# Three one-row reads between the loads and the stores of a rotary-embedding kernel

## The chip, the cores and the metric

One core of a Trainium2 chip runs the kernel. The metric is the device time of the program in microseconds; each kernel was run several times, always beside the kernel before on the same chip. All runs told of here are of the fast state. A ratio is the mean time of one kernel's fast runs over that of the other kernel's fast runs of the same rounds, so it is not quite the ratio of the medians that I quote. The profile of a kernel shows one of its executions; its span (83.6 us before) is shorter than the device time (85.28 us); it is counted from the program's first instruction to its last.

## The reference

```python
# x: [8, 8, 1024, 64] float32; cos_cached, sin_cached: [1024, 32] float32
half = x.shape[-1] // 2
x_first, x_second = x[..., :half], x[..., half:]
out_first  = x_first * cos_cached - x_second * sin_cached
out_second = x_first * sin_cached + x_second * cos_cached
return concatenate([out_first, out_second], axis=-1)
```

16.8 MB go in and 16.8 MB come out; the tables are 128 KB each.

## The kernel before

x is cut into 8 units of 128 partitions x 4096 floats (2 MB). All units have their own place in SBUF, so every load can be issued at once, and every store goes out from the place where its unit was loaded and computed. VectorE (DVE in the profiles) makes most of the products, GpSimd (POOL) and TensorE (PE) make most of the sums, ScalarE (ACT) copies into and out of PSUM. What the change touches is the list of SP, the engine that issues nearly all transfers. What SP has issued and the 16 DMA engines have yet to move is called its ring (q1 in the profiles):

```python
nc.sync.dma_start(out=rs, in_=sin_cached...)       # SP
nc.scalar.dma_start(out=rc, in_=cos_cached...)     # ACT, its own ring
for m0, m1 in ((0, F // 2), (F // 2, F)):          # unit 0 in two halves
    nc.sync.dma_start(out=xt[0][:, m0:m1], in_=xf[0][:, m0:m1])
for u in range(1, n_u):
    nc.sync.dma_start(out=xt[u], in_=xf[u])
# ... compute; as units are ready, in this order:
# store(0), store(1), ... store(6), then unit 7 in three parts
def store(u, n0=0, n1=R):
    nc.sync.dma_start(out=of[u][:, n0*hd:n1*hd], in_=xt[u][:, n0*hd:n1*hd])
```

The framework gives each of these transfers one of eight completion semaphores in turn. Before it reuses one it makes the issuing engine wait until the transfer eight places earlier has landed. The instruction lists of the traces show this wait at the issues; the source does not.

## Time and profile before

| | before |
|---|---|
| device time, median of the first 3 runs | 85.28 us (85.21 to 85.71) |
| span of the profile | 83.6 us |
| last load of x landed | 43.37 us |
| last compute instruction ended (POOL) | 75.5 us |
| last store landed | 82.62 us |
| share of 16 DMA engines' time used by SP's ring | 95.5% |

Read it from the bottom row up: the ring is what is full, and it still runs 7 us after the last engine has finished. The prediction below shows the lines. To them I add SP's own waits (columns: who waited, for whom, us in total, times, longest), of the kernel before (three dots: lines left out):

```profile
SPq L142 <- POOL w L110: 39.3, 8, 12.1
SPq L142 <- DVE w L106: 13.3, 3, 9.7
SPq L142 <- ACT w L190: 12.3, 2, 7.2
...
SPq L83 <- DMA w<-in_x_dram: 1.5, 1, 1.5
```

SP waits for most of the span, nearly always for compute (L142 is the store).

### The profile page before, as it was taken

Reading aid. Unit: us, or ns where it says so; the run is one execution under the profiler, and the core shown is the slowest. Engines: PE = TensorE matmul, PEld = TensorE weight load, DVE = VectorE, ACT = ScalarE, POOL = GpSimd, SP = SyncE. Lnnn points to the kernel's source line nnn. Section 1 sums busy time; section 2 is a strip of 40 time slices with the busy share of each in tenths; the row PEclk is TensorE's granted clock in tenths of the full one; section 3 lists DMA queues with packets and bytes.
Section 4 is the critical chain, followed back from the end, with each engine's and each line's share of the span. In section 5 each row is a group of like instructions: output and inputs, shape, how many; then the busy total and the mean of one; then the engine's idle time right before and its main releaser. Section 6 shows DMA issues by size and latency. Waiting matters only on the chain.

```text
span 83.6 us, 386 instructions
## 1 busy us (share of the span) xinstructions
PE 44.1 (53%) x80; PEld 16.9 (20%) x80; DVE 68.5 (82%) x30; ACT 40.7 (49%) x36; POOL 67.2 (80%) x36
## 2 busy tenths in 40 slices
PE   0199930004993694949769494961994970000000
PEld 0143300002430332405133240411340410000000
DVE  0193999999999999999999999999999998940000
ACT  4409694464068548196176856675266526000000
POOL 3009909999999999999999999999999999991000
PEclk9999999999999999999999999999579999655555
DMA  1999999999999999999999898999999999999990
GB/s 18 308 415 447 435 431 447 392 470 407 423 447 407 454 400 439 439 415 447 384 423 454 384 486 384 478 400 454 423 400 470 392 478 392 470 400 394 423 425 20
DMA packets 2833, 33.82 MB, mean 404 GB/s; under 512 B 337, under 2 KB 337, under 8 KB 785
## 3 DMA queue, kind: packets, MB, share of 16 engines
q1 hardware_dynamic: 2784, 33.69, 95.5%
q10 hardware_dynamic: 48, 0.13, 0.4%
q14 instruction: 1, 0.00, 0.0%
HBM read 17.04 MB, written 16.78 MB: 404 GB/s over the span
## 4 chain that ended last, share of the span: by engine, by line
POOL 63%; issue 13%; PE 4%; DMA 4%; DVE 3%; POOLq 2%
POOL w L109 26%; POOL w L110 24%; POOL w L106 14%; PE en L156 4%; DMA w<-in_sin_cached_dram 4%; DVE w L106 3%; POOLq L258 2%; POOLq L109 0%; POOLq L106 0%
## 5 line engine op out<-in xcount | busy, mean ns | idle before, releaser
L106 DVE TENSOR_TENSOR w<-st,tb 128x3072 f32<-128x3072 f32 (+2 forms) x19 | 54.7, 2956 | 0.3 <-ACT st L113 0.3
L113 ACT COPY st<-w 128x1536 f32<-128x1536 f32 (+1 forms) x19 | 24.9, 1310 | 15.7 <-DVE w L106 14.6
L184 PE MATMUL acc<-w,plus 128*128 128x512 f32 x36 | 21.4, 679 | 20.4 <-ACT w L190 11.4
L109 POOL TENSOR_TENSOR w<-w 128x1024 f32<-128x1024 f32 (+3 forms) x11 | 23.9, 2169 | 0.2
L110 POOL TENSOR_TENSOR w<-w 128x1024 f32<-128x1024 f32 (+3 forms) x11 | 23.8, 2166 | 0.0
L184 PEld LDWEIGHTS acc<-w,plus 128*128 128x128 f32 x36 | 6.9, 215 | 33.9 <-ACT w L190 18.0
L190 ACT COPY w<-acc 128x1024 f32<-128x1024 f32 x9 | 9.1, 1010 | 8.5 <-PE acc L185 8.5
L106 POOL TENSOR_TENSOR w<-w,tb 128x1280 f32<-128x1280 f32 x4 | 11.7, 2921 | 0.2
L185 PE MATMUL acc<-w,minus 128*128 128x512 f32 x18 | 10.9, 690 | 0.0
L185 PE MATMUL acc<-w,plus 128*128 128x512 f32 x18 | 9.2, 592 | 0.0
L162 POOL COPY tb<-tb 32x2048 f32<-32x2048 f32 x2 | 3.8, 1888 | 5.2 <-DVE tb L159 5.2
L156 PE MATMUL en<-w,sel 32*128 32x512 f32 x4 | 3.7, 1089 | 3.9 <-DMA w<-in_sin_cached_dram 3.9
L185 PEld LDWEIGHTS acc<-w,minus 128*128 128x128 f32 x18 | 4.0, 223 | 5.4 <-issue 5.4
L106 DVE TENSOR_TENSOR w<-pre,tb 128x4096 f32<-128x4096 f32 x1 | 4.4, 4418 | 0.0
L185 PEld LDWEIGHTS acc<-w,plus 128*128 128x128 f32 x18 | 3.4, 190 | 4.4 <-issue 4.4
L109 POOL TENSOR_TENSOR w<-w,w 128x1024 f32<-128x1024 f32 x1 | 2.4, 2361 | 2.2 <-issue 2.2
L156 PE MATMUL ec<-w,sel 32*128 32x512 f32 x4 | 3.6, 1056 | 0.0
L160 ACT COPY tb<-tb 32x2048 f32<-32x2048 f32 x1 | 1.9, 1897 | 3.4 <-DVE tb L159 3.4
L106 DVE TENSOR_TENSOR w<-w,en 128x2048 f32<-128x2048 f32 x1 | 2.3, 2289 | 1.4 <-PE en L156 1.4
L159 DVE LOAD_MASK_SELECT tb<-w x2 | 0.0, 8 | 3.8 <-DMA w<-in_sin_cached_dram 3.8
L159 DVE STREAM_SHUFFLE tb<-w 32x1024 f32<-32x1024 f32 x2 | 2.5, 1282 | 0.0
L106 DVE TENSOR_TENSOR w<-w,ec 128x1024 f32<-128x1024 f32 x2 | 2.4, 1218 | 0.0
(18 smaller groups left out, 14.2 us busy)
## 6 DMA issues: line engine op xcount, KB each, us to landing
w<-in_x_dram SPq DMA_DIRECT2D x7, 2048.0 KB, 24.9
out_dram<-w SPq DMA_DIRECT2D x7, 2048.0 KB, 10.5
w<-in_x_dram SPq DMA_DIRECT2D x2, 1024.0 KB, 6.4
out_dram<-w SPq DMA_DIRECT2D x2, 768.0 KB, 6.7
out_dram<-w SPq DMA_DIRECT2D x1, 512.0 KB, 6.7
w<-in_cos_cached_dram ACTq DMA_DIRECT2D x1, 128.0 KB, 3.3
w<-in_sin_cached_dram SPq DMA_DIRECT2D x1, 128.0 KB, 3.1
```

Source lines behind the costliest of these rows:

```text
L106: eng.tensor_tensor(out=o, in0=a, in1=t, op=TT.mult)
L109: eng.tensor_tensor(out=o[:, :, 0], in0=c[:, :, 0], in1=s[:, :, 1], op=TT.subtract)
L110: eng.tensor_tensor(out=o[:, :, 1], in0=c[:, :, 1], in1=s[:, :, 0], op=TT.add)
L113: nc.scalar.copy(out=pt[:, :(n1 - n0) * hd], in_=xt[u][:, n0 * hd:n1 * hd])
L156: nc.tensor.matmul(part, sel, r, start=True, stop=True)
L159: nc.vector.stream_shuffle(t[0:Q, H:], flat(r), odd)
L160: nc.scalar.copy(out=tb4[Q:2 * Q, H:], in_=tb4[0:Q, H:])
L162: nc.gpsimd.tensor_copy(out=tb4[k * Q:(k + 1) * Q, H:], in_=tb4[0:Q, H:])
L184: nc.tensor.matmul(a[:, k], plus, xr[:, :, k], start=True, stop=False)
L185: nc.tensor.matmul(a[:, k], plus if k else minus, sr[:, :, 1 - k], start=False, stop=True)
L190: nc.scalar.copy(out=rows(xt[u], n0, n0 + G), in_=a)
L258: with _tile.TileContext(nc) as tc:
```

## The change

The three reads bring a row of 64 floats each into a small buffer that nobody uses. They do no work for the result. They cost three small transfers and shift the semaphores of all stores by three places.

```diff
     for u in range(1, n_u):
         nc.sync.dma_start(out=xt[u], in_=xf[u])
+
+    row = const.tile([1, 3 * hd], fp32, name="row")
+    for i in range(3):
+        nc.sync.dma_start(out=row[:, i * hd:(i + 1) * hd], in_=xf[i][0:1, 0:hd])
```

## The prediction

> **What bounds the kernel now.** I read the page first, from its DMA lines. They say that the queues are never empty.
>
> ```profile
> DMA  1999999999999999999999898999999999999990
> GB/s 18 308 415 447 435 431 447 392 470 407 423 447 407 454 400 439 439 415 447 384 423 454 384 486 384 478 400 454 423 400 470 392 478 392 470 400 394 423 425 20
> ...
> q1 hardware_dynamic: 2784, 33.69, 95.5%
> ...
> HBM read 17.04 MB, written 16.78 MB: 404 GB/s over the span
> ```
>
> Each digit is one fortieth of the span, 2.09 us. Apart from the first and the last slice the 16 DMA engines are busy in tenths 8 or 9 all the way, and SP's ring (q1) alone fills 95.5% of 16 engines' time. The chain of waits names another engine:
>
> ```profile
> POOL 63%; issue 13%; PE 4%; DMA 4%; DVE 3%; POOLq 2%
> ```
>
> That chain starts from the last instruction of a compute engine, and POOL's last work ends at 75.5 us of a span of 83.6 us. The stretch view shows what is left after that (columns: stretch, length, busy us of PE, PEld, DVE, ACT and POOL, granted clock, DMA share, GB/s):
>
> ```profile
> 43.00:48.00 5.00, 3.90 (x10) 1.62 (x9) 5.00 (x3) 3.57 (x4) 5.00 (x4) 1.00 0.98 419
> 53.00:58.00 5.00, 2.79 (x7) 0.95 (x5) 5.00 (x2) 3.52 (x3) 5.00 (x3) 1.00 1.05 449
> 63.00:68.00 5.00, 3.90 (x10) 1.44 (x8) 5.00 (x3) 2.36 (x2) 5.00 (x3) 1.00 0.98 419
> 73.00:78.00 5.00, 0.00 (x0) 0.00 (x0) 1.15 (x2) 0.00 (x0) 2.51 (x2) 0.50 0.99 423
> 78.00:82.60 4.60, 0.00 (x0) 0.00 (x0) 0.00 (x0) 0.00 (x0) 0.00 (x0) 0.50 0.81 334
> ```
>
> From 78 us on no compute engine works, and the DMA engines still run until 82.6 us. The bound is therefore the transfer stream: 9 loads of x, then 10 stores, on one ring. The compute engines matter only if they hand a store over so late that the ring runs dry. The issues of the stores and their times to landing say whether they do:
>
> ```profile
> 21.76 0.35 SPq L142 DMA_DIRECT2D out_dram<-w  x1
> 35.39 0.34 SPq L142 DMA_DIRECT2D out_dram<-w  x1
> 47.90 0.33 SPq L142 DMA_DIRECT2D out_dram<-w  x1
> 63.90 0.33 SPq L142 DMA_DIRECT2D out_dram<-w  x1
> 69.51 0.33 SPq L142 DMA_DIRECT2D out_dram<-w  x1
> 75.53 1.35 SPq L142 DMA_DIRECT2D out_dram<-w  x2
> ```
> ```profile
> DMA to landing us min/median/max: 5.8/9.5/26.4
> ```
>
> The store issued at 21.76 us takes 26.4 us to land although 2 MB need only about 4.9 us: it stands behind the loads. From the trace's records of the completion semaphores I take each landing. Loads of unit 0 (two halves) 6.62 and 9.10, units 1 to 7 at 13.99, 18.88, 23.78, 28.67, 33.57, 38.46, 43.37 us; stores of units 0 to 6 at 48.20, 53.12, 58.04, 62.96, 67.89, 72.80, 77.70 us; the three parts of unit 7 at 79.54, 81.38, 82.62 us. That is one full transfer each 4.89 us (loads) or 4.92 us (stores), without a hole. A store is issued before the one ahead of it has landed by: 43.37 - 21.76 = 21.6, 48.20 - 35.39 = 12.8, 53.12 - 47.90 = 5.2, 5.5 (issue 52.51), 5.8 (57.12), 4.0 (63.90), 3.3 (69.51), 5.7 (72.03), 4.0 (75.53), 5.4 us (75.96). The smallest slack is 3.3 us, at unit 6. A new transfer needs about 1.1 us from issue to its first packet (the sine table: issue 0.74, first packet 1.79), so some 2.2 us of it are real.
>
> **What the Trainium skill says.** "DMA: Bandwidth & Descriptors", section "Anatomy of one DMA": the DMA engines do not wait on semaphores; a wait is held by the issuing sequencer before dispatch. The trace agrees: SP's waits stand ahead of its issues, and loads that were issued by 6.96 us move until 43.37 us. Same page, "Queues, rings and completion order": on each DMA engine descriptors are consumed in ring order. The 26.4 us of the first store agree. Same page, "Specifications": a fabric ceiling of 435 GB/s for 16 engines. Here 2.097 MB in 4.89 us is 429 GB/s, so there is nothing to gain from more in flight. Same page, "Why a DMA increments its semaphore by 16 and not by 1": a transfer runs on k engines, k at most 16 and set by the slowest dimension that is not 1. A row of 64 elements may then go as one 256 B packet on one engine or as 16 pieces of 16 B; no record of the kernel before shows which.
>
> **The change part by part.** Nothing is removed. The compute engines have the same instructions in the same order, with the same waits. SP's list gains three issues after the ninth load, and the completion semaphores are shifted by that: there are eight, handed out in the order of issue (the cosine table on ACT's queue included), and each issue first waits for the transfer eight places earlier. 21 transfers become 24.
>
> (a) Waits before the reads. They wait for the second half of unit 0 (9.10 us), unit 1 (13.99) and unit 2 (18.88), so SP issues them then. SP has nothing else to do: its first store is ready at 21.76 us. Cost 0.
>
> (b) Waits before the stores. Before, the stores of units 0 to 4 waited for the loads of the second half of 0, then 1 to 4. Now they wait for the loads of units 3, 4, 5, 6 and 7, landing at 23.78, 28.67, 33.57, 38.46 and about 43.4 us. Against the issue times 21.76, 35.39, 47.90, 52.51 and 57.12 us only the first is held up, by 23.78 - 21.76 = 2.0 us, and that store has 21.6 us of slack. The stores of units 5 and 6 and the first part of 7 wait for the three reads (landed by about 44 us; issues at 63.90, 69.51, 72.03). The last two parts wait for the stores of units 0 and 1, as before (landed 48.2 and 53.1; issues 75.5 and 76.0). Cost 0.
>
> (c) Bytes in the ring. The reads are issued after the last load (6.63 us) and so lie between it and the first store, at about 43 us, in the stream that sets the end. The trace's packets give the size: 4096 B take 159 ns, 16384 B 611 ns (medians), so 452 ns for 12288 B, or 0.0368 ns a byte, and 159 - 151 = 8 ns fixed. A 256 B packet is then an estimated 8 + 9.4 = 17 ns, its semaphore packet 9 ns (mean of the 4 B packets), 26 ns a read, 3 x 26 = 0.08 us on the busiest engine. All ten stores move back by that.
>
> (d) Overhead between transfers. Eight 16 KB packets per engine are 8 x 611 = 4.89 us, and loads follow each other every 4.89 us; a boundary costs less than 0.03 us. Stores, at 4.92 us, bound it by 0.03 us. Three more boundaries: at most 0.09 us.
>
> (e) Memory. The row's buffer takes 768 B per partition and moves the x buffers up by that. Bytes, shapes and engines stay the same: I put it at 0.
>
> The sum is 0.08 to 0.17 us. 85.28 + 0.12 = 85.40 us.
>
> **The rivals.** First: small transfers do not overlap like large ones. At the end of a transfer some 0.7 us pass from the semaphore packets' start to its landing (the sine table: 16 packets between 2.4 and 3.2 us, landing 3.80). If each read had to finish before the next packet of its engine could move, this would be about 3 x 0.7 = 2.1 us: 87.4 us, just slower by over 2%. For it: the kernel before has no transfer as small in its ring, so no row excludes it. Against it: the same latency ends every large transfer, and no boundary shows it. A part of it, say 0.5 us, seems possible.
>
> Second: the shifted waits hold SP's in-order list and the ring runs dry. This needs a store later by over 2.2 us of real slack at unit 6, or over 20 us at unit 0. The latest landing that any of them newly waits for is about 44 us, 20 us ahead of the issue it guards. Only if a read landed after 64 us would this be slower, by the delay itself. I hold it to be very unlikely.
>
> Third: POOL's chain is the true bound and the ring only follows. Then the reads would cost nothing at all, and the time would be 85.28 us. No compute instruction waits for a store, so a later ring cannot slow POOL.
>
> Fourth: a gain, if holding the first store back eased the loads. But that store does not move before 43 us in either kernel, so I see no path to one.
>
> **Range and chances.** The three runs of before spread over 0.5 us (85.21 to 85.71), which is more than the effect. The low end is that scatter below the lowest run, 85.0; the high end leaves room for half of the first rival, 86.3. Faster by over 2% (below 83.6) 1%, within 2% 95%, slower (above 87.0) 4%, which is the first rival whole.
>
> **What would show it.** Right: three issues of row at about 9.1, 14.0 and 18.9 us; the first store at 23.8 instead of 21.8 us and the second at 35.4; the DMA digits unbroken around 43 us; the store of unit 0 landing at 48.3 us, and each later one 0.1 us later than before; POOL ending at 75.5 us. Wrong: a dip to tenths 7 or less in the slices around 43 to 46 us, or the store of unit 0 landing after 49 us, would speak for the first rival; a store of units 2 to 7 issued late with SP waiting for a DMA, for the second. A different packet time of the 16 KB packets would mean that the moved buffers matter after all, which I left out.

## The result, and the profile after

| | before | after |
|---|---|---|
| median of 6 runs | 85.28 us (85.18 to 85.71) | 85.06 us (84.90 to 85.29) |
| ratio, 95% interval | | 0.9972, 0.9949 to 0.9996 |
| first store issued | 21.76 us | 23.92 us |
| second store issued | 35.39 us | 35.52 us |
| last load of x landed | 43.37 us | 43.42 us |
| store of unit 0 landed | 48.20 us | 48.35 us |
| last store landed | 82.62 us | 82.46 us |

The kernels are the same within 2%; the 0.28% by which the changed one was faster is looked at below. The profile after: the DMA digits and the ring's share from the page, then the three reads among the DMA issues.

```profile
DMA  2999999999999999999999999999999999999992
...
q1 hardware_dynamic: 2790, 33.69, 96.2%
...
row<-in_x_dram SPq DMA_DIRECT2D x3, 0.2 KB
```

The digits are unbroken. The ring has 2790 packets where it had 2784: six more for three reads. So each read is one data packet and one semaphore packet on a single DMA engine, and not 16 pieces on 16 engines. The trace's packet records show the three data packets at 42.90 to 42.94 us, right behind the loads, 18 ns each, and each semaphore packet takes 9 ns.

SP's list in the profile after, from narrow stretches of the timeline (start, length, operation):

```profile
9.19 0.29 SPq L88 DMA_DIRECT2D row<-in_x_dram  x1
14.07 0.23 SPq L88 DMA_DIRECT2D row<-in_x_dram  x1
18.95 0.22 SPq L88 DMA_DIRECT2D row<-in_x_dram  x1
23.92 0.38 SPq L147 DMA_DIRECT2D out_dram<-w  x1
35.52 0.37 SPq L147 DMA_DIRECT2D out_dram<-w  x1
```

And SP's waits after:

```profile
SPq L147 <- POOL w L115: 34.1, 7, 12.1
...
SPq L88 <- DMA w<-in_x_dram: 11.4, 3, 4.6
...
SPq L147 <- DMA w<-in_x_dram: 4.7, 1, 4.7
```

The reads wait 11.4 us for loads in all, and one store, the first, now waits for a load. These are new waits of 16 us together that cost nothing that can be seen: SP would have stood waiting for compute in that time (its waits for POOL, DVE and ACT at the stores fall from 64.9 to 48.1 us together). The first store's semaphore waited for unit 3's load, the store was issued 2.2 us later than before, and its first packet started at 42.6 us in either kernel.

### The profile page after: what moved, and what is told of

Its sections match the earlier page's. It is cut to its first block, busy times and chain, and to the rows that moved or that the text cites. A ratio compares the mean times of both kernels' runs of the same rounds, so it can differ in the third digit from the quotient of the medians.

```text
span 83.3 us, 389 instructions
## 1 busy us (share of the span) xinstructions
PE 44.3 (53%) x80; PEld 16.8 (20%) x80; DVE 68.5 (82%) x30; ACT 40.8 (49%) x36; POOL 67.1 (80%) x36
## 3 DMA queue, kind: packets, MB, share of 16 engines
q1 hardware_dynamic: 2790, 33.69, 96.2%
## 4 chain that ended last, share of the span: by engine, by line
POOL 64%; issue 13%; PE 5%; DMA 4%; DVE 3%; POOLq 2%
POOL w L115 26%; POOL w L114 24%; POOL w L111 14%; PE en L161 5%; DMA w<-in_sin_cached_dram 4%; DVE w L111 3%; POOLq L263 2%; POOLq L114 0%; POOLq L111 0%
## 5 line engine op out<-in xcount | busy, mean ns | idle before, releaser
L189 PE MATMUL acc<-w,plus 128*128 128x512 f32 x36 | 21.5, 682 | 20.2 <-ACT w L195 11.2
```

The source lines that it names most:

```text
L189: nc.tensor.matmul(a[:, k], plus, xr[:, :, k], start=True, stop=False)
```

## The experiments

The theory (A): the ring is the bound; a wait on SP costs only when it lets the ring run dry; small transfers in a full ring cost their packets. Rivals: a held store is lost time (W); only what is in the ring counts, not the wait (R); POOL's chain sets the end (P). Beside them stood the small gain to be explained.

### The small gain: four kernels, five rounds each

All four in one batch of rounds. Control: the kernel before, unchanged.

> The kernel before, unchanged, timed against itself: it says how large a ratio is that means nothing. All theories expect 1.000; if the ratio is off by 0.2% or more, or its interval excludes 1, the 0.28% gain measured for the change (0.9972) is no more than what two loads of the same program can show.

Measured: 85.30 us, beside 85.26 us, ratio 1.0002 (0.9984 to 1.002). Differences of 0.2% are the edge of what five rounds can tell.

The changed kernel again, no edit.

> The changed kernel once more, on the same chip as the other three. Theory A (my prediction: the reads cost under 0.1 us in the ring, nothing else changes): 1.000 to 1.002. Theory B (the 0.28% gain is real, from the buffers that moved by 768 B or from the reads themselves): 0.996 to 0.998 again.

Measured: 85.12 us, ratio 0.9987 (0.9964 to 1.001).

Only the address shift:

```diff
     row = const.tile([1, 3 * hd], fp32, name="row")
-    for i in range(3):
-        nc.sync.dma_start(out=row[:, i * hd:(i + 1) * hd], in_=xf[i][0:1, 0:hd])
```

> The row buffer is allocated, so the x buffers move by 768 B, but the three reads are gone. If the address shift makes the gain: 0.997. If the reads make it: 1.000. If it is scatter: within what the control shows.

Measured: 85.34 us, ratio 1.0015 (0.9991 to 1.004). The buffers' new addresses do not make a gain.

Only the reads, their buffer allocated behind the x buffers:

```diff
-    row = const.tile([1, 3 * hd], fp32, name="row")
+    row = xp.tile([1, 3 * hd], fp32, name="row")
```

> The three reads at the same place in SP's list, but their buffer lies behind the x buffers, which stay where they were. If the address shift makes the gain: 1.000 to 1.002. If the reads make it (by letting the slowest DMA engine, which ended 0.23 us after the next in the kernel before and 0.04 us after it in the changed one, catch up): 0.997. If it is scatter: within what the control shows. Theory A on the reads: 256 B packets of 18 ns near 42.9 us, first store issued at 23.9 us.

Measured: 85.12 us, ratio 0.9982 (0.9964 to 1.000). First store issued at 23.75 us, data packets of 18 ns at 42.70 to 42.74 us, as theory A has it. The gain, if it is one, goes with the reads; the interval touches 1.

### Six, seven, eleven reads: when the shifted wait starts to bite

From here to the reads on ACT's list every kernel had three rounds. Six:

```diff
-    row = const.tile([1, 3 * hd], fp32, name="row")
-    for i in range(3):
+    row = const.tile([1, 6 * hd], fp32, name="row")
+    for i in range(6):
```

> Six rows are read in place of three. The first store now waits for the load of unit 6 (landing 38.5 us), the second for unit 7 (43.4 us). Theory A (the ring is the bound, a wait costs only when it lets the ring run dry): both lie ahead of the ring's need, so 1.000 +- 0.003, although the first store is issued 16.7 us later than in the kernel before and the second 8 us later. Rival W (a store that is held is time lost): several per cent slower.

Measured: 85.46 us beside 85.30 us, ratio 1.0016 (0.999 to 1.0041). SP's list in this kernel:

```profile
38.56 0.38 SPq L147 DMA_DIRECT2D out_dram<-w  x1
43.56 0.37 SPq L147 DMA_DIRECT2D out_dram<-w  x1
```

The first store came 16.8 us later than in the kernel before, the second 8.2 us later, and no loss is clear of noise (0.41% at the most). Rival W, which expected several per cent, falls.

Seven: the same edit with 7 in place of 6.

> One read more than the six. Now the first store waits for the load of unit 7, the last one in the ring, which lands at 43.4 us, some 0.5 us after its last packet. Theory A: the first store is issued at 43.5 us, its first packet follows about 1.05 us later (as for the sine table), so the ring is empty from 43.0 to about 44.5 us; every store and the end move back by 1.5 to 1.6 us: 86.8 us, ratio about 1.018. Rival R (the time of the small reads is what counts, not the wait): one more read is one more 27 ns, ratio as with six. Rival P (POOL's chain sets the end): no change either, as POOL waits for no store.

Measured: 87.06 us (87.04 to 87.10), ratio 1.0209 (1.0187 to 1.023): clearly slower, though unclear against the mark of 2%, and about 1.8 us over the 85.30 us beside it. One more read of 256 B costs 1.6 us (87.06 against 85.46 us). Its list, and its stretches round the turn from loads to stores (stretch, length, busy us of PE, PEld, DVE, ACT and POOL, granted clock, DMA share, GB/s), then the same stretches of the kernel with six reads:

```profile
43.29 0.38 SPq L147 DMA_DIRECT2D out_dram<-w  x1
43.84 0.37 SPq L147 DMA_DIRECT2D out_dram<-w  x1
```
```profile
42.00:43.00 1.00, 0.53 (x1) 0.30 (x2) 1.00 (x1) 1.00 (x2) 1.00 (x2) 1.00 0.56 231
43.00:44.00 1.00, 1.00 (x4) 0.51 (x3) 1.00 (x2) 0.38 (x2) 1.00 (x1) 1.00 0.00 0
44.00:45.00 1.00, 1.00 (x4) 0.44 (x3) 1.00 (x1) 1.00 (x1) 1.00 (x2) 1.00 1.25 524
```
```profile
42.00:43.00 1.00, 0.35 (x1) 0.30 (x2) 1.00 (x1) 1.00 (x2) 1.00 (x2) 1.00 1.13 477
43.00:44.00 1.00, 1.00 (x3) 0.38 (x2) 1.00 (x1) 0.51 (x1) 1.00 (x1) 1.00 0.97 410
44.00:45.00 1.00, 1.00 (x4) 0.48 (x3) 1.00 (x2) 0.87 (x1) 1.00 (x2) 1.00 0.99 426
```

From 43 to 44 us nothing moves with seven reads, and everything moves with six. (Packets are counted by their start, so a share can pass 1.) The first store here waits for the last load. When that has landed, the ring has been empty for half a microsecond already, and the store's own first packet comes 0.9 us after its issue. By the packet records the last load packet ends at 42.71 us and the first store packet starts at 44.16 us: a hole of 1.45 us, where I had expected 1.5 to 1.6. Against the profile of the kernel before, the store of unit 0 landed 1.43 us later (49.63 us, not 48.20) and the last store 1.59 us later (84.21 us, not 82.62). What makes the medians differ by 0.2 us more is not shown; it is no more than the scatter of the stores' pace, which takes 4.92 us a full store in these two profiles and 4.86 us in the changed kernel's, 0.3 us over six intervals. Compute went on unhindered in the hole (DVE and POOL 1.00 of 1.00 us), POOL's last work ended at 75.45 us as before (75.51), and the end moved all the same: rivals R and P fall.

Eleven, of half rows for room:

```diff
+    row = const.tile([1, 11 * half], fp32, name="row")
+    for i in range(11):
+        nc.sync.dma_start(out=row[:, i * half:(i + 1) * half], in_=xf[i % 8][0:1, 0:half])
```

> Eleven reads, of half rows (128 B, for room). The ninth to eleventh wait for the landing of the first to third (43.5, 43.7 and 43.9 us in the changed kernel, 0.19 us apart), each takes 0.25 us to issue, and the first store waits for the fourth (44.1 us). Theory A: first store issued at about 44.5 us, its first packet at 45.5 us, the ring empty but for the small reads for 2.5 us: 87.6 to 87.9 us, ratio 1.028 to 1.032. Rival R: eleven reads of 27 ns, 0.3 us, ratio at most 1.004.

Measured: 87.29 us, ratio 1.0233 (1.021 to 1.0255), slower by the mark of 2%, but below my 1.028. The first store was issued at 44.15 us, not 44.5, since the early reads landed sooner than I had thought and SP's issues of 0.25 us each alone set the pace. The hole runs from 42.60 to 45.03 us by the packet records, 2.43 us, as large as expected. The loads before it took 611 ns a packet in that profile where most others have 613 to 615 (medians), and the last load's first semaphore packet started at 42.21 us, 0.3 us ahead of the changed kernel's 42.55: that gives back most of the difference in that profile. The direction is theory A's, the size is not settled to better than 0.4 us.

### Wider reads: bytes in the ring

```diff
+    row = xp.tile([P, 9 * hd], fp32, name="row")
+    for i in range(3):
+        nc.sync.dma_start(out=row[:, 3*i*hd:3*(i+1)*hd], in_=xf[i][:, 0:3*hd])
```

> Three reads at the same place with the same waits, but each of 768 B on all 128 partitions (98 KB), behind the x buffers. Theory A: 8 packets an engine and read, each 8 + 768 x 0.0368 = 36 ns by the line through the 4 KB and 16 KB packets, so 0.29 us a read and 0.9 us for three: 86.2 us, ratio 1.010. Rival P (POOL's chain sets the end): 1.000. Rival L (every small transfer costs a fixed latency): no more than the three rows, 1.000.

Measured: 86.20 us (85.94 to 86.83), ratio 1.0121 (1.008 to 1.0163). The 384 data packets took 36 ns each in the median, as reckoned (mean 39). Three reads of 24 such packets an engine in all, and three semaphore packets, are 24 x 36 + 3 x 9 = 891 ns, 1.05% of the time. The ring charges the reads for their bytes and packets; a fixed latency for each transfer would have cost these three no more than three rows, and the six rows above cost 0.41% at the most.

### Other places for the same three reads

At the head of SP's list:

```diff
+    row = const.tile([1, 3 * hd], fp32, name="row")
+    for i in range(3):
+        nc.sync.dma_start(out=row[:, i * hd:(i + 1) * hd], in_=xf[i][0:1, 0:hd])
     rs, rc = sv[3][0:Q, 0:C], sv[3][0:Q, C:2 * C]
     nc.sync.dma_start(out=rs, in_=sin_cached...)
```

> The same three reads of one row, first on SP's list instead of between loads and stores. Theory A: they wait for nothing, but each takes SP 0.3 to 0.4 us to issue, at a time when SP is what the ring waits for, so the sine table and all of x start 1.0 to 1.2 us later, and so does the end: 86.2 to 86.5 us, ratio 1.012 to 1.014. Rival R (only bytes in the ring count): 0.1 us, 1.001.

Measured: 86.29 us beside 85.26 us, ratio 1.0114 (1.0089 to 1.014). SP's list, and the DMA lines of the page:

```profile
0.74 0.34 SPq L77 DMA_DIRECT2D row<-in_x_dram  x1
1.41 0.24 SPq L77 DMA_DIRECT2D row<-in_x_dram  x1
1.70 0.33 SPq L80 DMA_DIRECT2D w<-in_sin_cached_dram  x1
```
```profile
DMA  1699999999999999999979999999999999999991
GB/s 52 173 403 426 465 434 426 442 419 442 426 442 426 411 442 419 434 419 434 403 295 442 419 434 411 434 434 426 442 426 442 419 442 419 434 434 388 430 420 72
```

The sine table is issued at 1.70 us instead of 0.74, and slice two shows the ring half awake (173 GB/s; 308 in the kernel before). But the size has another make-up than I said. x's first half landed at 7.12 us, only 0.5 us later than before. That fits the cosine table being out of the way by then: on ACT's ring its packets ended at 2.40 us here and at 3.19 us before; no run tries it alone. The other 0.6 us of this profile come with slow packets at the last load of x (slice 21, 295 GB/s), of which more below. So the ratio is a little below the 1.012 that I expected, and half of it is not explained.

On ACT's list:

```diff
-        nc.sync.dma_start(out=row[:, i * hd:(i + 1) * hd], in_=xf[i][0:1, 0:hd])
+        nc.scalar.dma_start(out=row[:, i * hd:(i + 1) * hd], in_=xf[i][0:1, 0:hd])
```

> The same three reads issued by ACT right after the cosine table. In this build they take completion semaphores ahead of most loads, so they wait for nothing and are issued from 1.2 us on, on ACT's ring beside SP's. Theory A: SP's issues are not delayed, the packets are 3 x 27 ns on one engine, ACT's list is held up for about 1 us; its copy of the selection matrix ends at 3.8 to 4.0 us instead of 3.0, about when the sine table lands (3.8 us): ratio 1.000 to 1.003. Rival H (three more transfers at the start cost the same wherever they are issued): as with the reads at the head of SP's list, 1.012.

Measured: 85.06 us, ratio 0.9974 (0.9952 to 0.9995). ACT's list in that profile:

```profile
1.19 1.09 ACTq L88 DMA_DIRECT2D row<-in_x_dram  x3
2.31 1.28 ACT L94 ACT_TABLE_LOAD   x1 [2.31 <-issue]
3.60 0.30 ACT L94 COPY sel<-plus 32x128 f32<-32x128 f32 x1
```

ACT is held for 1.1 us and ends its copy at 3.9 us. My "SP's issues are not delayed" holds for the tables and the first three loads of x only. The others take over other semaphores by the shift and wait for them: unit 2 is issued at 4.10 us, not 2.59, and unit 7 at 7.43 us, not 6.63. The ring had enough to do, and the loads landed no later (the last at 43.29 us, before at 43.37). Rival H falls: at the start, the three issues cost 1.1% on the list that feeds the ring and nothing on the other. Here too the kernel was faster by a quarter of a per cent, without any read between loads and stores, and with every store waiting for the same transfers as in the kernel before.

### What the last 0.3% are made of: a theory that fell

The packet records show something that the pages hardly show (a 7 in slice 21 with the reads at the head). In many profiles a number of 16 KB load packets that start between 40 and 43.4 us take 640 to 1350 ns instead of 611 to 615. The kernel before has ten of them, up to 982 ns; the changed kernel's profile has none, but the profile of its second build, of a run of 85.46 us where four of the other five took 85.07 to 85.14, has 26. The theory (T): a store queued behind the loads disturbs their end, by an amount that differs from run to run. Two kernels to try it, five rounds each, the first with the load of unit 7 in two parts:

```diff
-    for u in range(1, n_u):
+    for u in range(1, n_u - 1):
         nc.sync.dma_start(out=xt[u], in_=xf[u])
+    for m0, m1 in ((0, 2560), (2560, F)):
+        nc.sync.dma_start(out=xt[7][:, m0:m1], in_=xf[7][:, m0:m1])
```

> No reads; the load of unit 7 goes as two parts of 10 KB and 6 KB a partition. The first store is issued at 21.8 us as in the kernel before. This is the control of the next run. In ten profiles so far with the first store queued behind the last load, nine have 16 KB load packets of 640 to 1350 ns (normal 611 to 615) between 40 and 43 us; the changed kernel's profile was the tenth, with none, and is the faster by 0.2 us there. The two with that store issued after 43 us have none. Theory T (the slow packets come of a store queued behind loads, differ from run to run, and are what the 0.1 to 0.3% differences are made of): slow packets again near 41 us; ratio 1.000 +- 0.003.

Measured: 85.65 us (85.34 to 86.19) beside 85.23 us, ratio 1.004 (0.9993 to 1.0087). The first store was issued at 21.80 us, as in the kernel before, yet no load packet of the profile is slow near 41 us (the 10 KB packets took at most 396 ns, normal 389).

The same with six reads (as above) behind it:

> The same split and six reads of one row: by the eight places the first store now waits for the first part of unit 7's load, so it is issued at about 41.6 us, 1.3 us before the ring's loads end, and its first packet can follow at 42.65 us without a hole. Theory A: no hole, so no loss, 1.000 or below. Theory T: no load packet over 640 ns between 39 and 42 us, since no store is queued then; the runs lie closer together, and the ratio is 0.996 to 0.999, the version to keep if it is clear of noise. If the slow packets are still there, they belong to the end of the loads and not to a queued store, and theory T falls. If the first store's packets start after 43.2 us, the hole shows and the ratio is above 1.003.

Measured: 85.64 us (85.45 to 85.91), ratio 1.003 (0.9992 to 1.0069). The first store was issued at 41.41 us, there was no hole and no load packet near 41 us as slow as meant here (one 10 KB packet took 496 ns), and no gain either.

Theory T falls as I put it: a queued store did not bring the slow packets in the one kernel, and their absence did not bring the time down in the other. That split loads behave differently from whole ones is possible and untested. What decides over these packets stays open. Nor do they make the difference between the two main profiles: there the last load landed at 43.37 us before and at 43.42 us after, and the 0.16 us at the end come from the stores, which need 29.50 us before and 29.19 us after from unit 0's landing to unit 6's. That time differs from profile to profile whether there are reads or not: 29.18 us with the shift only, 29.46 us with the reads only. So the small gain stays open too: four measurements of three kernels with three small reads lie at 0.9972 to 0.9987, two of these intervals exclude 1 by at most 0.0005, and the kernel with six reads lies at 1.0016. The address shift is not its cause; no more is shown. No version here beats the kernel before by more than that.

## Why the prediction was right

The range held; the predicted 85.40 us is 0.34 us above the median, and the small difference points the other way, within what runs scatter. The range (85.0 to 86.3 us) is many times the 0.08 to 0.17 us of the working, so that it held says little by itself; the parts and the experiments say more. Step by step, by its letters:

- **(a), waits before the reads, cost 0.** Right. Issues at 9.19, 14.07 and 18.95 us, each within 0.1 us of the figure given; SP had nothing to do then.
- **(b), waits before the stores, cost 0.** Right, and the experiments show the reason rather than the outcome alone. With six reads the first two stores are held by 17 and 8 us at no cost; with seven, where the first store waits for the last load itself, 1.8 us are lost. The prediction's bound for that store, a delay of over 20 us, is about right: 16.8 us cost nothing, 21.5 us (43.29 - 21.76) do. The prediction's second rival is a real mechanism that three reads do not reach. It named a dry ring as the condition, which is right; the slack that it worked out at the later stores was never touched. Its 1.1 us from issue to first packet were 0.9 us for the store behind the hole.
- **(c), packets in the ring, 0.08 us.** Right in its parts: 18 ns measured against 17, 9 ns for the semaphore, on one engine. The wide reads show the same line through packet sizes at a size that can be seen in the time.
- **(d), boundaries, at most 0.09 us.** No cost was seen, but so small a one could not be. "All ten stores move back by that", said under (c), did not come out: the store of unit 0 landed 0.15 us later than before, the last one 0.16 us earlier. The stores of that profile ran at 4.86 us each, not 4.92. The working is also weaker than it looks: 611 ns is the median of all 16 KB packets, but the loads of that profile have 615 ns, and 8 x 615 ns are 4.92 us, more than the 4.89 us from load to load. A bound of 0.1 us drowns in what the packets do by themselves.
- **(e), the moved buffers, 0.** Right: 1.0015 with an interval that holds 1, and the 16 KB packets have the same medians in both profiles (loads 615 ns, stores 611).
- **The first rival**, a latency per small read, falls: six reads cost no more than 0.4% by the upper end of their interval, where 0.7 us each would be 4.2 us. The trace's semaphore times speak against it too: in the changed kernel the last read landed at 43.92 us, in the middle of the first store's packets, which had not waited for it. (The "2.4 and 3.2 us" behind its 0.7 us take in the cosine table's packets; the sine table's 16 semaphore packets start between 2.36 and 2.93 us.) **The third rival**, POOL as the bound, falls by the hole of the seven reads, in which POOL worked on and the end moved. **The fourth**, a gain, I gave no path. The runs lean to one of 0.1 to 0.3%, and I have no path for it now.

## What to carry to other kernels

Where one ring is full from end to end, ask of every new wait whether it empties the ring, not how long it is: holding the first store back by 17 us was free, and holding it until half a microsecond after the last load's packets cost 1.8 us. Adding a transfer, however small, shifts the semaphore reuse of every later one, so look at which earlier landing each issue now waits for, above all at the turn from loads to stores. Put such transfers where the issuing list has nothing to feed; the same three reads at its head cost 1.1%, of which the late start explains about half.

## What the Trainium skill lacked or had wrong

- No page has the cost of reusing completion semaphores in turn on one issuing list. Here, with eight of them, it decides which landing an issue comes to wait for: 1.0016 when the first store waits for the last load but one, 1.0209 when it waits for the last.
- "DMA: Bandwidth & Descriptors", section "Rules for kernel authors", says that transfers under 64 KB pay mostly overhead, but not what that overhead comes to behind a full ring. Here a 256 B read took 18 + 9 ns of one DMA engine; about 9 of these 27 ns are bytes (an estimate from the line through the 4 KB and 16 KB packets), so the share agrees with the page. Six such reads left the ratio at 1.0016.
- No page tells of load packets that slow down at the end of a run of loads: 16 KB packets of 640 to 1350 ns in place of 611 to 615, starting between 40 and 43.4 us, in nine of the first twelve profiles. Their cause is open.
- No page gives a scatter for the packet time itself: medians of 611 to 615 ns for 16 KB, changing between profiles and between loads and stores. For the 64 such packets that each DMA engine moves in half of this kernel that is about 0.26 us (an estimate, 64 x 4 ns), more than the change that was studied.
